# Weight-sum tables built in half-size pieces, one transfer at a time, in a two-layer decoder trunk on one core

## The chip, the core and the metric

The kernel runs on one core of a Trainium2 chip. The core has a matrix engine (TensorE, PE in the profile, with its weight loads listed as PEld), a vector engine (VectorE, DVE), a scalar engine (ScalarE, ACT), a general engine (GpSimd, POOL) and an engine that only issues transfers (SyncE, SP). Each runs its own list of instructions in order, and they meet through semaphores. Data comes from the chip's memory (DRAM) through 16 DMA engines, which all queues share: SP's transfers go through the queue that the profile calls q1, POOL's through q0.

The metric is the device time of one execution in microseconds, the median of several runs. Before the change it is 1178.66 us (three runs, 1177.95 to 1180.91).

## What is computed

The reference is a decoder trunk of two layers on 512 tokens of 1024 features, all in 32-bit floats. Layer 0 mixes with attention (8 forgetting-attention heads and 8 stick-breaking heads), layer 1 with a gated short convolution; each is followed by a gated MLP. Cut to its core:

```python
def conv_ffn(h, norm_g, w_up, conv_w, w_down):
    xn = rms_norm(h, norm_g)
    u = causal_dwconv(xn @ w_up, conv_w)
    g, val = u[..., :D_FF], u[..., D_FF:]
    return (jax.nn.silu(g) * val) @ w_down

def reference(x, ...):
    h = x
    for layer in range(DEPTH):              # DEPTH = 2
        i = layer // 2
        if layer % 2 == 0:
            h = h + attention_mixer(h, ...)
        else:
            h = h + short_conv_mixer(h, ...)
        h = h + conv_ffn(h, ffn_norm[layer], ffn_w_up[layer], ffn_conv[layer], ffn_w_down[layer])
    return h
```

`attention_mixer` is an input projection (`attn_w_in`, 1024 by 3080), normed queries and keys, two kinds of attention and an output projection (`attn_w_out`). D_FF is 2816, so `ffn_w_up` is 1024 by 5632.

## The kernel before

The program is one long stretch for each stage: attention (to about 300 us), the first MLP, the convolution mixer, the second MLP. Activations stay in SBUF; weights stream in from DRAM.

**Weights in attention.** `weights()` hands out the next weight tile (512 KB: 1024 rows by 128 columns, or 512 by 256). `load` has three buffers for the raw tile (`raw`) and three for its two halves `whi` and `wlo`, into which ACT (line 290) and DVE (line 291) split it, since each product is made of three passes of rounded halves (lines 311 to 313 for queries, keys and output). SP issues the load (line 284) as soon as a raw buffer is free, two tiles ahead of use. Heads and projections are woven together: a unit of a head (`logits`, `turn`, `weigh`, lines 605 to 830) alternates with pieces of the projections for later heads (`fillers`).

**Weights in the MLP.** The up projection multiplies 2 by 2 blocks of the matrix with seven products in place of eight (`Sevens`, line 1042 and around it). Some of these products need sums of weight blocks, named by the products p7, p6 and q4: the sum for p7 is the lower right block plus the upper right one, p6's is that plus the upper left, q4's that plus the lower left. For the second MLP these are added up on chip. For the first, columns 2 to 10 (groups of 256) have their sums ready in DRAM tables: nine tables, three sums (`"7"`, `"6"`, `"4"`) by three chunks of three groups, each 512 rows by 768 columns, 1.5 MB.

**How the tables are made.** `table_steps` is a generator that POOL's transfers come from. A step is one transfer from DRAM to DRAM: a plain copy (line 101), from the weights or from the table before, or a copy that adds onto what is there (line 99, `accum_op`). Six steps make the three tables of a chunk: copy and add for 7, copy and add for 6, copy and add for 4. The generator is called once ahead of attention's loop and then once a unit, and `pin` keeps its transfers in the order of the program among POOL's instructions. The scheduler puts the semaphores: a step waits until the step whose rows it reads or adds to has landed, and each eighth POOL transfer shares a counter.

**Who reads them.** In the first MLP, SP loads the 7 sum of a group into `Y` (line 1058), and the 6 and 4 sums into raw buffers (line 1066). POOL's next work behind the tables is a transfer that adds a block onto the tile `X` (line 1069), one for each group.

The loop that calls the generator, in the program of before:

```python
    sums_far = table_steps()
    next(sums_far)
    fill(PRE)
    for g in range(len(units) + 2):
        next(sums_far, None)
        if g < len(units):
            waiting[g] = logits(*units[g])
            fill(FILL1)
```

Of the kernel before, what the change touches and what calls it, by code (L numbers as in the profile page):

```python
# [22 lines left out]
ALU = mybir.AluOpType  # L23
# [26 lines left out]
CHUNKS = (2, 3), (5, 3), (8, 3)  # L50
# [4 lines left out]
def trunk(  # L55
# [6 lines left out]
    nc = tc.nc  # L62
# [20 lines left out]
    tables = {}  # L83

    def table_steps():

        w = ffn_w_up[0]
        for n in "764":
            for g, m in CHUNKS:
                tables[n, g] = far.tile([512, m * 256 + 16], F32, tag=f"t{n}{g}", name=f"t{n}{g}")  # L90
        def block(kh, half, g, m):
            return w[kh * 512:(kh + 1) * 512, half * DFF + g * 256:half * DFF + (g + m) * 256]
        for step in range(6):
            n = "764"[step // 2]
            for g, m in CHUNKS:
                to = tables[n, g][:, 0:m * 256]
                if step % 2:
                    src = block(*((0, 1), (0, 0), (1, 0))[step // 2], g, m)
                    pin(nc.gpsimd.dma_start(to, src, accum_op=ALU.add))
                else:  # L100
                    pin(nc.gpsimd.dma_start(to, block(1, 1, g, m) if step == 0 else tables["76"[step // 2 - 1], g][:, 0:m * 256]))
                yield

    def table_of(n, group):
        g, m = next(c for c in CHUNKS if c[0] <= group < c[0] + c[1])
# [120 lines left out]
    def fill(us):  # L226
        quota[0] += us
        while quota[0] > 0 and fillers:
            before = clock[0]
            if next(fillers[0], None) is None:  # L230
                fillers.pop(0)
            quota[0] -= clock[0] - before
# [15 lines left out]
    brought, pin = {}, tc.keep_in_program_order  # L248
# [486 lines left out]
    def turn(p, b, w):  # L735


        n = (b + 1) * P
        if b == 0:
            pts[p] = [aw.tile([P, 20, P], F32R, tag=f"pt{i}", name=f"pt{p}{i}", bufs=1) for i in range(2)]  # L740
        if b < 2:
            t = bank("c")
            for e in range(2):
                for k in range(b + 1):
                    c = (e * (b + 1) + k) * P
                    pe.transpose(t[:, c:c + P], w[:, e, k * P:(k + 1) * P], ident)
            src = t[:, 0:2 * n].rearrange("p (e n) -> p e n", e=2)
            if b:
                hi, lo = (t_[:, 4:20, :].rearrange("p (e k) q -> p e (k q)", e=2)[:, :, P:3 * P] for t_ in pts[p])
            else:  # L750
                hi, lo = (t_[:, 0:20:19, :] for t_ in pts[p])
            act.activation(hi, src, AF.Copy)
            dve.tensor_tensor(lo, src, f32(hi), op=ALU.subtract)
        else:
            for e in range(2):
                t = bank("c")
                for k in range(b + 1):
                    pe.transpose(t[:, k * P:(k + 1) * P], w[:, e, k * P:(k + 1) * P], ident)
                to = (5 * b, 19 - 6 * b)[e]
                hi, lo = (t_[:, to:to + b + 1, :].rearrange("p k q -> p (k q)") for t_ in pts[p])  # L760
                act.activation(hi, t[:, 0:n], AF.Copy)
                dve.tensor_tensor(lo, t[:, 0:n], f32(hi), op=ALU.subtract)
        spend(0.22 * (b + 1))

    def weigh(p):

        need(("v", p // 2))
        v = v_tiles[p // 2]  # L770
        if p == 4:
            o_tiles[1] = mixed(1)
        o_hi, o_lo = o_tiles[p // 4]
        total = work.tile([P, S], F32, tag="y", name=f"o{p}")
        for e in range(2):
            acc = bank("a")
            for k in range(NB):
                w = v[:, k, 2 * (p % 2) + e].rearrange("p i d -> p (i d)")
                first, step = ((6 * k, 5), (1 + k, 6))[e]
                out_ = acc[:, k * P:] if e == 0 else acc[:, 0:(NB - k) * P]  # L780
                for i, t in enumerate(pts[p]):
                    pe.matmul(out_, w, t[:, first:first + step * (NB - k - 1) + 1:step, :], start=k == 0 and i == 0, stop=k == NB - 1 and i == 1)  # L782
            src = acc.rearrange("p (b q) -> p b q", q=P)
            if e:
                src = src[:, ::-1, :]
            own, other = (slice(i * HD, (i + 1) * HD) for i in (e, 1 - e))
            to = total[own, :].rearrange("p (b q) -> p b q", q=P)
            act.activation(to, src[other], AF.Copy)
            dve.tensor_tensor(to, src[own], to, op=ALU.add)
            spend(1.2)  # L790
        split(o_hi[:, p % 4, :], o_lo[:, p % 4, :], total)

    def output(g, done):
        o_hi, o_lo = o_tiles[g]
        for o in range(ND):
            if o % 2 == 0:
                w = weights()
            acc = bank("a")
            c = slice((o % 2) * P, (o % 2 + 1) * P)
            for k in range(4):  # L800
                mm3(acc, (w[0][:, k, c], w[1][:, k, c]), (o_hi[:, k, :], o_lo[:, k, :]), k == 0, k == 3)
                yield 1
            done(o, acc)
# [15 lines left out]
    def output_begin():  # L819
        last_w.append([weights(), weights(AHEAD - 1)])  # L820
        yield from output_part(range(4), range(2), "b")
        last_w.append([weights(AHEAD - 1), weights(0)])
        yield from output_part(range(4), (2,), "b")
# [19 lines left out]
    rows = {}  # L843
# [95 lines left out]
    units = [(p, u) for p in range(8) for u in range(len(UNITS))]  # L939
    waiting = {}  # L940
    sums_far = table_steps()
    next(sums_far)
    fill(PRE)
    for g in range(len(units) + 2):
        next(sums_far, None)
        if g < len(units):
            waiting[g] = logits(*units[g])
            fill(FILL1)
        if g == len(units):
            fillers.append(output_begin())  # L950
            fill(BEFORE)
        if g >= 2 and units[g - 2][1] == len(UNITS) - 1:
            p = units[g - 2][0]
            weigh(p)
            if p == 3:
                fillers.append(output(0, residual))
        if 1 <= g <= len(units):
            for b, w in waiting.pop(g - 1):
                turn(units[g - 1][0], b, w)
                fill(FILL2 / len(UNITS[units[g - 1][1]]))  # L960
# [42 lines left out]
    class Blocks:  # L1003
# [15 lines left out]
        def block(self, name, k0, nk):  # L1019
            return self.at(k0 + (HF if name in "cd" else 0), nk)[:, :, LEFT if name in "ad" else RIGHT]  # L1020
# [662 lines left out]
```

## Time and profile before

| | |
|---|---|
| median of three runs | 1178.66 us (1177.95 to 1180.91) |
| the profiled execution | 1180.35 us, its span 1177.6 us |
| PE busy | 1132.7 us, 96% of the span |
| DVE, ACT, POOL busy | 949.4, 676.1, 138.8 us |
| mean granted clock of PE | 0.98 of full speed |
| moved by POOL's queue | 71.74 MB of 189.40 MB |
| chain that ended last | PE 82%, DMA 8%, DVE 4%, issue 2%, ACT 2% |

The profile comes from one execution. Its page cuts the span into 40 slices of 29.4 us and shows the busy share of each engine in tenths, the clock that PE was granted, and how full the DMA engines were. An answer by windows gives the same for chosen stretches in microseconds. An answer on waits says which engine stood still for whom. In an answer in order of time each row has its start and length, and in brackets the idle time before it with what ended it. "To landing" is the time from a transfer's issue to its last semaphore.

### The profile page before, as it was taken

Reading aid. Unit: us, or ns where it says so; the run is one execution under the profiler, and the core shown is the slowest. Engines: PE = TensorE matmul, PEld = TensorE weight load, DVE = VectorE, ACT = ScalarE, POOL = GpSimd, SP = SyncE. Lnnn points to the kernel's source line nnn. Section 1 sums busy time; section 2 is a strip of 40 time slices with the busy share of each in tenths; the row PEclk is TensorE's granted clock in tenths of the full one; section 3 lists DMA queues with packets and bytes.
Section 4 is the critical chain, followed back from the end, with each engine's and each line's share of the span. In section 5 each row is a group of like instructions: output and inputs, shape, how many; then the busy total and the mean of one; then the engine's idle time right before and its main releaser. Section 6 shows DMA issues by size and latency. Waiting matters only on the chain.

```text
span 1177.6 us, 19211 instructions
## 1 busy us (share of the span) xinstructions
PE 1132.7 (96%) x7619; PEld 1018.4 (86%) x7619; DVE 949.4 (81%) x1447; ACT 676.1 (57%) x1006; POOL 138.8 (12%) x156
## 2 busy tenths in 40 slices
PE   8987479999999999999999999999999999999998
PEld 7875358877888999999999889998888999998886
DVE  5764258988689978788998897885699899898886
ACT  7542246766456676667655644544354676766654
POOL 4101100000000111001420001000001111113300
PEclk9988689999999999999999999999999999999999
DMA  6799981212235787769994327543356786779961
GB/s 190 236 235 252 278 194 53 72 37 72 72 90 156 205 212 188 195 188 306 194 229 148 88 92 167 138 123 93 90 152 123 173 180 157 161 226 225 221 170 54
DMA packets 171401, 189.40 MB, mean 161 GB/s; under 512 B 6860, under 2 KB 140540, under 8 KB 171312
## 3 DMA queue, kind: packets, MB, share of 16 engines
q1 hardware_dynamic: 131712, 116.37, 32.1%
q0 software_dynamic: 39440, 71.74, 31.7%
q8 instruction: 59, 0.97, 0.3%
q14 instruction: 30, 0.25, 0.1%
q10 hardware_dynamic: 160, 0.07, 0.0%
HBM read 183.18 MB, written 30.41 MB: 181 GB/s over the span
## 4 chain that ended last, share of the span: by engine, by line
PE 82%; DMA 8%; DVE 4%; issue 2%; ACT 2%; another core or an unknown queue 1%; SPq 0%; DVEq 0%; ACTq 0%; POOLq 0%
PE psb L1042 23%; PE psb L1595 10%; PE psa L1042 9%; PE psa L1595 8%; DMA raw<-in_attn_w_in 7%; PE psb L311 5%; PE psb L313 4%; PE psb L312 4%; PE psa L311 3%; PE psa L313 3%; PE psa L312 3%; PE psa L782 2%; DMA Xc<-in_conv_w_in 1%; PE psb L686 1%; DVE wlo L291 1%
## 5 line engine op out<-in xcount | busy, mean ns | idle before, releaser
L290 ACT ACTIVATE whi<-raw 128x1024 fp32r<-128x1024 f32 (+2 forms) x93 | 95.9, 1033 | 140.4 <-DMA raw<-in_attn_w_in 51.0
L291 DVE TENSOR_TENSOR wlo<-raw,whi 128x1024 fp32r<-128x1024 f32 (+2 forms) x93 | 110.5, 1189 | 70.1 <-ACT whi L290 69.3
L1042 PE MATMUL psb<-p_lo,whi_p 128*128 128x256 f32 x408 | 115.0, 282 | 0.0
L1042 PE MATMUL psb<-p_hi,wlo_p 128*128 128x256 f32 x408 | 114.9, 282 | 0.0
L1042 PE MATMUL psb<-p_hi,whi_p 128*128 128x256 f32 x408 | 114.8, 281 | 0.0
L311 PE MATMUL psb<-hs_a,whi 128*128 128x512 f32 x240 | 101.1, 421 | 6.0 <-ACT qk L656 6.0
L313 PE MATMUL psb<-hs_a,wlo 128*128 128x512 f32 x240 | 97.0, 405 | 0.0
L1042 PEld LDWEIGHTS psb<-p_hi,whi_p 128*128 128x128 f32 x408 | 77.3, 190 | 0.0
L1042 PEld LDWEIGHTS psb<-p_lo,whi_p 128*128 128x128 f32 x408 | 76.9, 189 | 0.0
L1042 PE MATMUL psa<-p_hi,wlo_p 128*128 128x256 f32 x272 | 76.8, 282 | 0.0
L1042 PE MATMUL psa<-p_lo,whi_p 128*128 128x256 f32 x272 | 76.7, 282 | 0.0
L1042 PE MATMUL psb<-q_lo,whi_q 128*128 128x256 f32 x272 | 76.6, 282 | 0.0
L1042 PEld LDWEIGHTS psb<-p_hi,wlo_p 128*128 128x128 f32 x408 | 76.6, 188 | 0.0
L1042 PE MATMUL psb<-q_hi,wlo_q 128*128 128x256 f32 x272 | 76.6, 281 | 0.0
L1042 PE MATMUL psb<-q_hi,whi_q 128*128 128x256 f32 x272 | 76.5, 281 | 0.0
L1042 PE MATMUL psa<-p_hi,whi_p 128*128 128x256 f32 x272 | 76.5, 281 | 0.0
L1069 POOL DMA_DIRECT2D X<-in_ffn_w_up x17 | 22.3, 1313 | 375.3 <-DVE wlo_p L992 274.2
L1595 PE MATMUL psb<-act,whi 128*128 128x256 f32 x352 | 63.3, 282 | 0.0
L311 PEld LDWEIGHTS psb<-hs_a,whi 128*128 128x128 f32 x240 | 46.8, 195 | 16.3 <-ACT qk L656 6.4
L421 DVE SCALAR_TENSOR_TENSOR uv<-yv,taps,uv 128x511 f32<-128x511 f32 (+1 forms) x84 | 59.8, 746 | 0.2
L421 DVE SCALAR_TENSOR_TENSOR ug<-yg,taps,ug 128x511 f32<-128x511 f32 (+1 forms) x84 | 58.9, 747 | 0.3 <-ACT ug L418 0.3
L1595 PE MATMUL psb<-whi,act 128*128 128x512 f32 x176 | 56.6, 398 | 0.0
(480 smaller groups left out, 3678.3 us busy)
## 6 DMA issues: line engine op xcount, KB each, us to landing
t<-in_ffn_w_up POOLq DMA_DIRECT2D x12, 1536.0 KB, 20.4
raw<-in_attn_w_in SPq DMA_DIRECT2D x24, 512.0 KB, 5.8
raw<-in_ffn_w_up SPq DMA_DIRECT2D x20, 512.0 KB, 3.9
t<-t POOLq DMA_DIRECT2D x6, 1536.0 KB, 19.1
X<-in_ffn_w_up SPq DMA_DIRECT2D x17, 512.0 KB, 5.0
W<-in_ffn_w_up SPq DMA_DIRECT2D x17, 512.0 KB, 4.7
X<-in_ffn_w_up POOLq DMA_DIRECT2D x17, 512.0 KB, 7.5
Z<-in_ffn_w_up SPq DMA_DIRECT2D x17, 512.0 KB, 4.4
```

The lines of the kernel that those rows point to most:

```text
L290: return (act.activation(hi[:, at_], raw[:, at_], AF.Copy), dve.tensor_tensor(lo[:, at_], raw[:, at_], f32(hi[:, at_]), op=ALU.subtract))
L291: dve.tensor_tensor(lo[:, at_], raw[:, at_], f32(hi[:, at_]), op=ALU.subtract))
L311: made = [pe.matmul(acc, w[0], rhs[0], start=first, stop=False), pe.matmul(acc, w[0], rhs[1], start=False, stop=False), pe.matmul(acc, w[1 ...
L312: pe.matmul(acc, w[0], rhs[1], start=False, stop=False),
L313: pe.matmul(acc, w[1], rhs[0], start=False, stop=last)]
L421: dve.scalar_tensor_tensor(dst[:, d:], src[:, 0:S - d], tap(j), dst[:, d:], op0=ALU.mult, op1=ALU.add)
L686: pe.matmul(ss[e][:, c:c + wide], ql[rows, b * P:n], kl[rows, 0:wide], start=first and b == bs[0], stop=last and b == bs[-1])
L782: pe.matmul(out_, w, t[:, first:first + step * (NB - k - 1) + 1:step, :], start=k == 0 and i == 0, stop=k == NB - 1 and i == 1)
L1042: pe.matmul(to, w[a][:, k, c], x[b][:, k, :], start=fresh and i + k + t == 0, stop=i == 1 and k == 3 and t == 2, skip_group_check=not fresh)
L1069: tc.keep_in_program_order(nc.gpsimd.dma_start(self.st[g][n], self.block_of(g, kh, half), accum_op=ALU.add))
L1595: pe.matmul(to, l, r, start=begin and o + t == 0, stop=end and t == 2 and o == (0 if layer else 1), skip_group_check=not fresh)
```

## The change

The same nine tables are made with the same sums. Each transfer now covers 256 of a table's 512 rows (0.75 MB), so there are 36 in place of 18. The loops change places: before, a step was made for all three chunks before the next step; now all six steps are made for the upper rows of a chunk, then for its lower rows, then the next chunk follows. In this order each transfer but the first of six reads or adds to what the one in front of it wrote. The loop over attention's units asks for two steps a turn.

```diff
-        for step in range(6):
-            n = "764"[step // 2]
-            for g, m in CHUNKS:
-                to = tables[n, g][:, 0:m * 256]
-                if step % 2:
-                    src = block(*((0, 1), (0, 0), (1, 0))[step // 2], g, m)
-                    pin(nc.gpsimd.dma_start(to, src, accum_op=ALU.add))
-                else:
-                    pin(nc.gpsimd.dma_start(to, block(1, 1, g, m) if step == 0 else tables["76"[step // 2 - 1], g][:, 0:m * 256]))
-                yield
+        for g, m in CHUNKS:
+            for rows in (slice(0, 256), slice(256, 512)):
+                for step in range(6):
+                    n = "764"[step // 2]
+                    to = tables[n, g][rows, 0:m * 256]
+                    if step % 2:
+                        src = block(*((0, 1), (0, 0), (1, 0))[step // 2], g, m)
+                        pin(nc.gpsimd.dma_start(to, src[rows, :], accum_op=ALU.add))
+                    else:
+                        src = block(1, 1, g, m) if step == 0 else tables["76"[step // 2 - 1], g][:, 0:m * 256]
+                        pin(nc.gpsimd.dma_start(to, src[rows, :]))
+                    yield
...
     for g in range(len(units) + 2):
-        next(sums_far, None)
+        for _ in range(2):
+            next(sums_far, None)
         if g < len(units):
```

## The prediction, made before the result was known

> **What bounds the kernel now.** I read the slices of the page first, then the waits of the worst stretch, the chain, the DMA queues, and last GpSimd's (POOL's) own order of time. The slices, each 29.4 us wide:
>
> ```profile
> span 1177.6 us, 19211 instructions
> ...
> PE   8987479999999999999999999999999999999998
> ...
> PEclk9988689999999999999999999999999999999999
> DMA  6799981212235787769994327543356786779961
> ```
>
> The kernel is bound by TensorE (PE) almost everywhere; the one hole is in slices 2 to 5, about 60 to 177 us. There the DMA engines are full and, with PE's busy share, its granted clock falls. Three stretches, before, in and after the hole (columns: length, busy time of PE, PEld, DVE, ACT and POOL with the number of instructions, granted clock, DMA share, GB/s):
>
> ```profile
> 40.00:68.00 28.00, 28.00 (x174) 22.10 (x173) 22.88 (x61) 15.12 (x33) 5.54 (x7) 1.00 1.04 281
> 68.00:180.00 112.00, 77.41 (x463) 61.98 (x463) 51.30 (x126) 40.17 (x92) 10.30 (x12) 0.79 1.00 239
> 180.00:306.00 126.00, 123.37 (x806) 101.87 (x803) 109.15 (x224) 81.80 (x160) 0.00 (x0) 1.00 0.19 58
> ```
>
> All three are the same attention code (heads, value projections, fillers). In the second PE is idle 112.00 - 77.41 = 34.6 us, in the third 126.00 - 123.37 = 2.6 us, or 2.1%. DVE and ACT are busy less than half of the second stretch, so neither is its limit. The waits of 68 to 180 us (who waited for whom, us in total, times, longest):
>
> ```profile
> ACT whi L290 <- DMA raw<-in_attn_w_in: 51.0, 5, 12.9
> PE psc L605 <- ACT sq L648: 9.1, 1, 9.1
> PE psb L686 <- ACT w L704: 8.0, 2, 7.7
> PE psc L638 <- DVE pt L762: 7.0, 1, 7.0
> PE psb L311 <- ACT qk L656: 6.0, 1, 6.0
> ```
>
> ACT splits every weight tile (line 290), works in order, and stands 51 us in front of tiles that have not landed; PE's waits name what is queued on ACT and DVE behind that split. The chain of work that ended last says it more plainly (start, us, what):
>
> ```profile
> 46.05 25.32 DMA raw<-in_attn_w_in
> ...
> 95.93 46.89 DMA raw<-in_attn_w_in
> ```
>
> A weight tile of 0.5 MB is on the chain for 47 us. The DMA queues of 46 to 172 us, when the tables are made, and then the loads of 180 to 306 us, when none are:
>
> ```profile
> q0 software_dynamic: 7013, 27.16, 89.0%
> q1 hardware_dynamic: 8291, 4.70, 15.7%
> ...
> t<-in_ffn_w_up POOLq DMA_DIRECT2D x9, 1536.0 KB, 22.3
> t<-t POOLq DMA_DIRECT2D x6, 1536.0 KB, 19.1
> raw<-in_attn_w_in SPq DMA_DIRECT2D x9, 512.0 KB, 44.5
> ```
> ```profile
> raw<-in_attn_w_in SPq DMA_DIRECT2D x4, 512.0 KB, 3.8
> ```
>
> The table transfers (queue q0) and the weight tiles (q1) move nearly the same number of packets, 7013 against 8291, but 27.16 MB against 4.70. The engines take turns packet by packet, and q0's packets are large (27.16 MB / 7013 = 3.9 KB, against 0.6 KB). With q0 never empty, a tile lands after 44.5 us (median) instead of 3.8, and nine tiles in 126 us is one in 14. So the hole is the weight tiles' queue behind tables that nobody needs before 355 us.
>
> **The change, part by part.** POOL's order before, from the first table on (DMASWn is a counter that every eighth POOL transfer raises; a transfer waits for its own counter's last use and for its data):
>
> ```order
> L101 DMA t_599<-in_ffn_w_up 512x768 [waits DMASW4_49]
> L101 DMA t_600<-in_ffn_w_up 512x768 [waits DMASW5_49]
> L101 DMA t_601<-in_ffn_w_up 512x768 [waits DMASW6_49]
> L99 DMA t_599<-in_ffn_w_up 512x768 [waits DMASW7_49,DMASW4_49]
> L99 DMA t_600<-in_ffn_w_up 512x768 [waits DMASW5_49,DMASW0_49]
> ```
>
> and after:
>
> ```order
> L103 DMA t_599<-in_ffn_w_up 256x768 [waits DMASW4_49]
> L100 DMA t_599<-in_ffn_w_up 256x768 [waits DMASW5_49,DMASW4_49]
> L103 DMA t_602<-t_599 256x768 [waits DMASW6_49,DMASW5_49]
> L100 DMA t_602<-in_ffn_w_up 256x768 [waits DMASW7_49,DMASW6_49]
> L103 DMA t_605<-t_602 256x768 [waits DMASW7_49,DMASW0_49]
> L100 DMA t_605<-in_ffn_w_up 256x768 [waits DMASW1_49,DMASW0_49]
> L103 DMA t_599<-in_ffn_w_up 256x768 [waits DMASW2_49]
> ```
>
> Three chunks were interleaved, so two transfers always stood behind the one under way. Now six steps on the same rows follow each other, and each waits for its predecessor's counter. Only the first of each later six (five places) has nothing to wait for but a counter long raised, and goes out with the one before. On PE, DVE, ACT and SP the rows stay the same, in the same order; on POOL 18 rows become 36. POOL in order of time before (start, us, what, idle before it and its releaser):
>
> ```profile
> 40.51 1.92 POOL L101 DMA_DIRECT2D t<-in_ffn_w_up  x3
> 49.87 1.11 POOL L99 DMA_DIRECT2D t<-in_ffn_w_up  x1 [7.44 <-DMA t<-in_ffn_w_up]
> 55.15 1.03 POOL L99 DMA_DIRECT2D t<-in_ffn_w_up  x1 [4.18 <-DMA t<-in_ffn_w_up]
> 60.56 1.01 POOL L99 DMA_DIRECT2D t<-in_ffn_w_up  x1 [4.38 <-DMA t<-in_ffn_w_up]
> 69.44 0.66 POOL L101 DMA_DIRECT2D t<-t  x1 [7.86 <-DMA t<-in_ffn_w_up]
> 77.83 0.64 POOL L101 DMA_DIRECT2D t<-t  x1 [7.74 <-DMA t<-in_ffn_w_up]
> 86.98 0.63 POOL L101 DMA_DIRECT2D t<-t  x1 [8.50 <-DMA t<-in_ffn_w_up]
> ...
> 142.87 1.00 POOL L99 DMA_DIRECT2D t<-in_ffn_w_up  x1 [3.14 <-DMA t<-t]
> 371.70 1.35 POOL L1069 DMA_DIRECT2D X<-in_ffn_w_up  x1 [227.82 <-DVE wlo_p L992]
> ```
>
> *How long the new chain takes.* With the queue full, copies land 5.3 us apart (49.87, 55.15, 60.56) and adds about 8.9 (60.56, 69.44, 77.83, 86.98). Halves then stream 2.65 and 4.45 us. The first copy was alone at its start: 49.87 - 40.51 = 9.4 us from issue to the next issue, less 5.3 of streaming: 4.1 us of fixed cost that the full queue hid and each wait now shows. So a pair is 2.65 + 4.45 + 2 x 4.1 = 15.3 us, eighteen pairs 275 us, less 5 x 4.1 where two go together: 255 us, from 40.5 to about 295 us instead of 170. No row shows the fixed cost of a lone half, so its bounds:
>
> ```profile
> spare<-in_ffn_conv POOLq DMA_DIRECT2D x4, 33.0 KB, 2.0
> ```
> ```profile
> p_lo_chain<-in_ffn_w_down POOLq DMA_DIRECT2D x6, 512.0 KB, 10.0
> ```
>
> Below, 2.0 us, a transfer of next to nothing: the chain ends at 40.5 + 128 + 31 x 2.0 = 230 us. Above, an add of 0.5 MB in the crowded down projection, 10.0 less a third of 8.9: 7.0 us, end at 385. I take 4.1, since it is the same transfer at the same place.
>
> *Who waits for POOL.* Until 371.70 nothing else of POOL is due. The last table is issued at 164 + 30F for a fixed cost F, 287 us with 4.1. The order shows the X transfer right behind it:
>
> ```order
> L103 DMA t_607<-t_604 256x768 [waits DMASW5_49]
> L100 DMA t_607<-in_ffn_w_up 256x768 [waits DMASW6_49]
> L1072 DMA X_3694<-in_ffn_w_up 128x4x256 [waits DMAHW7_49,DVE_49]
> ```
>
> It comes due about 45 us earlier than before, at 326, so POOL is free 39 us ahead. The tables' readers (first and last start):
>
> ```profile
> L1058 SPq DMA_DIRECT2D Y<-t x9: 367/499/508, 355.7 to 504.7; - x9
> ```
>
> Nine groups 18.6 us apart; the three chunks, first read at 356, 411 and 467, would be read at 311, 366 and 422 and be whole at about 128, 212 and 295. The halved transfers' own issues are free beside POOL's 227.82 us of idleness; only if the chain ran past 326 would that cover be gone.
>
> *What PE gets back.* First its idleness, 34.6 us. Then the clock: the five pieces of the hole at half clock are
>
> ```profile
> 72.73:79.55 6.82, 5.43 (x43) 4.20 (x44) 4.11 (x9) 3.94 (x12) 0.64 (x1) 0.52 1.09 214
> 106.90:117.10 10.20, 5.76 (x28) 4.63 (x29) 4.47 (x9) 3.26 (x7) 0.92 (x1) 0.51 1.09 213
> 123.90:134.20 10.30, 7.20 (x22) 5.09 (x23) 4.78 (x12) 4.93 (x13) 0.95 (x2) 0.51 1.05 348
> 137.60:151.20 13.60, 6.68 (x27) 5.33 (x28) 6.30 (x16) 5.94 (x12) 2.03 (x2) 0.51 1.05 236
> 164.90:171.70 6.80, 4.75 (x17) 3.99 (x17) 4.88 (x10) 2.96 (x9) 0.00 (x0) 0.52 0.98 258
> ```
>
> PE is busy 29.8 of these 47.7 us, and half of that, 14.9, is the clock's. Together 49.5; the work left, 112 - 49.5 = 62.5 us, keeps the 2.1% of the calm stretch: -1.3. The Trainium skill, TensorE: Matmul & The Clock Gate, Terms, sets the penalty at the throttled time times one half, which would put 23.9 us in place of 14.9 and end at 1125 us. The rows differ, because the remaining 17.9 us of those pieces are idle and counted already; I keep 14.9.
>
> *What the tiles still lose.* In each gap of 4.1 us q0 is empty, and a tile alone lands in 3.8; in a pair's 15.3 us that is two tiles, and the 7.1 us of streaming carry another half at one in 14. So a tile each 6 us at the least, where PE at full pace wants nine in 62.5 us, one in 7. A tile issued just as an add starts lands after about 4.45 + 3.8 = 8.3 us. Three buffers run ahead, but tiles come in bursts. Between nothing, as at 40 to 68 us, where PE never stood under a full queue, and 1 us for each of some 22 tiles up to 295 us, I take 3 us: nearer the lower end, since even 25.32 us of lateness cost little before 73 us.
>
> The saving is 34.6 + 14.9 - 1.3 - 3 = 45 us. The rest of the program only moves ahead. The profiled execution took 1180.35 us, 2.75 around its span; it becomes 1135. It lay 1.7 above the median shown, 1178.66; against that the forecast is 1134.
>
> **The rivals.** (a) *Half of it stays:* the tables crowd the tiles for 255 us rather than 130, and each of the 22 tiles costs its 1 us or more: 22 us in place of 3, about 1153. For it, the calm stretch now gets a rival queue; against it, the gaps. (b) *POOL comes late:* the chain's last issue at 164 + 30F reaches 326 at F = 5.4 us, after which X, and with it the weights of every group, are late by 30 us for each us of F. At 6.9 nothing is left of the saving, at 8 the kernel takes 1212. For it speaks the 10.0 us row; against it 9.4 us for twice the copy. The Trainium skill, SBUF — State Buffer, SBUF: two separate sides, says that certain VectorE operations lock GpSimd out while it writes descriptors, 620 ns becoming 3100; by that F would be 6.6 and the time about 1170. The issues at 40.51 took 1.92 for three beside a DVE busy 22.88 of 28 us, so the trace does not show it. (c) *The tables were not the cause:* ACT's and DVE's own chain binds 68 to 180 us, and the time stays near 1175; against it, the third stretch, 98% busy with the same code. (d) *The change doesn't do what it says:* the five pairs in flight make a full queue of 7.1 us at most, too little to matter.
>
> **How the numbers follow.** Forecast (1129 to 1142): 0.77. (a), 1142 to 1165: 0.13. (c): 0.03, of which 0.01 unmoved. (b): 0.07, of which 0.05 slower, 0.01 unmoved and 0.01 faster. (d): none. The range 1127 to 1156 takes the forecast and most of (a), since its loss is the term with no row. A change of 0.3%, 3.5 us, is about what can be told from none. Faster 0.93, same 0.02, slower 0.05.
>
> **What would show it.** Right: weight tiles landing in 4 to 9 us between 46 and 290 us, PE over 95% busy at full clock there, ACT's wait for raw under 8 us, tables issued until 280 to 300 us, and the first Y read from a table near 311 us. Wrong: POOL's last table after 326 us, or raw still over 15 us to landing.

## The result

The changed kernel takes 1131.07 us (median of four runs, 1129.42 to 1131.6) against 1178.31 us for the kernel before, measured beside it: a ratio of 0.9595 (95% interval 0.9574 to 0.9615), 47 us saved. The forecast was 1134 us, range 1127 to 1156. In the profiled execution the span went from 1177.6 to 1127.5 us.

The slices of the page after, each 28.2 us wide:

```profile
span 1127.5 us, 19238 instructions
...
PE   8999999999999999999999999999999999999998
...
PEclk9999999999999999999999999999999999999999
DMA  6678767674368777799953455543275876789961
```

The hole in slices 2 to 5 (counted from 0) is gone, the granted clock does not fall, and the DMA engines are busy six to eight tenths up to slice 8 instead of nearly full in slices 2 to 5. (Lines of the program after the edit stand two to three lower: the split of a weight tile, 290 and 291 before, is now 292 and 293, and the X transfer, 1069 before, is 1072.) The same stretches, with the columns of the prediction:

```profile
40.00:68.00 28.00, 28.00 (x173) 22.08 (x172) 23.03 (x62) 16.29 (x34) 4.14 (x6) 1.00 0.81 203
68.00:180.00 112.00, 111.42 (x794) 92.78 (x793) 93.21 (x225) 73.71 (x162) 13.35 (x18) 1.00 0.78 190
180.00:261.00 81.00, 78.37 (x487) 63.65 (x484) 68.31 (x127) 47.86 (x92) 9.68 (x13) 1.00 0.72 179
```

From 68 to 180 us PE runs 794 matmuls where it ran 463, and is idle 0.6 us where it was idle 34.6. The DMA queues of 46 to 172 us after:

```profile
q0 software_dynamic: 4346, 16.30, 57.7%
q1 hardware_dynamic: 11984, 6.82, 19.5%
...
raw<-in_attn_w_in SPq DMA_DIRECT2D x14, 512.0 KB, 5.0
```

In the same 126 us the tables move 16.30 MB instead of 27.16, and the weight tiles' queue 11984 packets instead of 8291. A tile lands after 5.0 us (median) instead of 44.5, and fourteen are fetched instead of nine. POOL in order of time, at the chain's start and end:

```profile
40.30 0.58 POOL L103 DMA_DIRECT2D t<-in_ffn_w_up  x1
46.94 0.99 POOL L100 DMA_DIRECT2D t<-in_ffn_w_up  x1 [6.05 <-DMA t<-in_ffn_w_up]
54.81 0.58 POOL L103 DMA_DIRECT2D t<-t  x1 [6.88 <-DMA t<-in_ffn_w_up]
59.50 0.99 POOL L100 DMA_DIRECT2D t<-in_ffn_w_up  x1 [4.11 <-DMA t<-t]
...
257.60 0.89 POOL L100 DMA_DIRECT2D t<-in_ffn_w_up  x1 [6.24 <-DMA t<-t]
323.37 1.35 POOL L1072 DMA_DIRECT2D X<-in_ffn_w_up  x1 [64.88 <-DVE wlo_p L995]
```

The last table is issued 66 us ahead of POOL's next work.

### The profile page after: what moved, and what is told of

Read it like the earlier page. It is cut to its first block, busy times and chain, and to the rows that moved or that the text cites. A ratio compares the mean times of both kernels' runs of the same rounds, so it can differ in the third digit from the quotient of the medians.

```text
span 1127.5 us, 19238 instructions
## 1 busy us (share of the span) xinstructions
PE 1116.9 (99%) x7619; PEld 1007.1 (89%) x7619; DVE 948.9 (84%) x1447; ACT 674.8 (60%) x1006; POOL 150.3 (13%) x174
## 4 chain that ended last, share of the span: by engine, by line
PE 90%; DVE 5%; ACT 2%; DMA 2%; issue 1%; DVEq 0%; ACTq 0%; POOLq 0%
PE psb L1045 23%; PE psb L1598 11%; PE psa L1045 9%; PE psa L1598 8%; PE psb L313 6%; PE psb L314 6%; PE psb L315 6%; PE psa L315 3%; PE psa L313 3%; PE psa L314 3%; DMA Xc<-in_conv_w_in 2%; PE psa L784 2%; PE psb L688 2%; PE psb L570 1%; PE psb L571 1%
## 5 line engine op out<-in xcount | busy, mean ns | idle before, releaser
L313 PE MATMUL psb<-hs_a,whi 128*128 128x512 f32 x240 | 98.5, 410 | 0.0
L1598 PEld LDWEIGHTS psb<-act,whi 128*128 128x128 f32 x352 | 54.2, 189 | 0.5 <-DVE act L995 0.3
L315 PEld LDWEIGHTS psb<-hs_a,wlo 128*128 128x128 f32 x240 | 45.1, 188 | 10.5 <-DVE wlo L293 0.2
```

The costliest lines, as they stand in the source:

```text
L313: made = [pe.matmul(acc, w[0], rhs[0], start=first, stop=False), pe.matmul(acc, w[0], rhs[1], start=False, stop=False), pe.matmul(acc, w[1 ...
L315: pe.matmul(acc, w[1], rhs[0], start=False, stop=last)]
L1598: pe.matmul(to, l, r, start=begin and o + t == 0, stop=end and t == 2 and o == (0 if layer else 1), skip_group_check=not fresh)
```

## The experiments

The change does three things at once: it halves the transfers, puts them chunk by chunk, and so leaves one in flight. The runs take these apart, and then ask what it is about the queue that delays a weight tile. All kernels keep the instructions of PE, ACT, DVE and SP in the same order; only POOL's table transfers differ. Each was timed beside the kernel before on the same chip.

**The changed kernel again.**

> The changed kernel once more, beside the variants on the same chip. Both theories: about 1131 us, ratio 0.96 to the kernel before; weight tiles land in about 5 us while the tables are made, and PE stays over 98% busy from 68 to 261 us.

Measured: 1130.62 us against 1177.74, ratio 0.9602 (0.9584 to 0.9619). It is the yardstick of the three that follow.

**The order alone, whole tables.** Against the changed kernel:

```diff
-            for rows in (slice(0, 256), slice(256, 512)):
+            for rows in (slice(0, 512),):
...
-        for _ in range(2):
-            next(sums_far, None)
+        next(sums_far, None)
```

> The new order alone: six steps on a chunk, each waiting for the one in front of it, but with whole tables of 1.5 MB, 18 transfers. Theory A (what counts is that POOL's queue runs empty between two transfers, and a weight tile gets through in that gap): the gap is there, only half as often; a copy and an add stream 13 us and leave two gaps of about 3 us, room for four tiles in 19 us. 1131 to 1138 us, tiles landing in 5 to 12 us, tables done near 210 us. Theory B (what counts is the size of a transfer, since a tile has to stand behind a whole one): a tile waits up to 9 us more behind an add, and a good part of the loss comes back: 1145 to 1165 us.

Measured: 1130.75 us, ratio 0.9606 (0.9589 to 0.9624): the whole saving, with transfers as large as before. Its DMA queues of 46 to 172 us and the stretch of 68 to 180 us:

```profile
q0 software_dynamic: 5100, 19.98, 64.8%
q1 hardware_dynamic: 11956, 6.80, 20.7%
...
raw<-in_attn_w_in SPq DMA_DIRECT2D x14, 512.0 KB, 7.9
```
```profile
68.00:180.00 112.00, 111.46 (x794) 92.81 (x792) 93.31 (x225) 73.67 (x162) 10.29 (x12) 1.00 0.88 218
```

Tiles land later, after 7.9 us, and it costs PE nothing. Theory B, that size decides, falls here.

**The halves alone, in the old order.** Against the changed kernel:

```diff
-        for g, m in CHUNKS:
-            for rows in (slice(0, 256), slice(256, 512)):
-                for step in range(6):
+        for step in range(6):
+            for g, m in CHUNKS:
+                for rows in (slice(0, 256), slice(256, 512)):
```

> The halves alone: 36 transfers of 0.75 MB in the old order, step by step over all three chunks, so that five more stand behind the one under way. Theory A: the queue never runs empty, tiles land after 40 us or more, the time is that of before, 1175 to 1182 us. Theory B: with half the size a tile waits half as long, and half of the saving is there, about 1155 us.

Measured: 1174.47 us, ratio 0.9971 (0.9960 to 0.9982), a saving of 3 us, half a microsecond beyond theory A's 1175 to 1182 and far from theory B's 1155.

```profile
q0 software_dynamic: 7301, 27.25, 87.4%
q1 hardware_dynamic: 9053, 5.09, 16.9%
...
raw<-in_attn_w_in SPq DMA_DIRECT2D x10, 512.0 KB, 40.7
```
```profile
68.00:180.00 112.00, 82.98 (x499) 66.84 (x497) 56.65 (x150) 43.68 (x100) 16.78 (x23) 0.82 0.98 238
```

The hole is back, with tiles at 40.7 us. So the halving by itself is worth 3 us, and the order by itself all of the saving.

**Two halves in flight.** Against the changed kernel:

```diff
-            for rows in (slice(0, 256), slice(256, 512)):
-                for step in range(6):
+            for step in range(6):
+                for rows in (slice(0, 256), slice(256, 512)):
```

> The halves of a chunk made side by side: upper rows and lower rows of each step, then the next step, so two transfers of 0.75 MB are in flight. Theory A: while one half's wait runs (about 3 us), the other streams (2.1 us a copy, 4.5 us an add), so the queue is empty only for a moment around the copies; tiles land in 12 to 30 us, tables done near 185 us, and 1145 to 1175 us. Theory B: transfers as small as in the changed kernel, so the time of the changed kernel, 1131 to 1136 us.

Measured: 1132.16 us, ratio 0.9616 (0.9601 to 0.9630). Theory A's number was wrong here: tiles landed after 9.1 us, not 12 to 30, and PE lost nothing. The number of theory B, 1131 to 1136 us, came out, although the two runs before had already refuted that size alone decides.

```profile
q0 software_dynamic: 6602, 24.87, 82.5%
q1 hardware_dynamic: 12018, 6.85, 19.0%
...
raw<-in_attn_w_in SPq DMA_DIRECT2D x14, 512.0 KB, 9.1
```

The tables are done at 189 us, not much later than the 170 of before. Either short empty moments are enough, or it is the amount in front of a tile that counts. The next two runs were meant to part these.

**Four quarters in flight**, as many bytes as two halves. Against the changed kernel:

```diff
-            for rows in (slice(0, 256), slice(256, 512)):
-                for step in range(6):
+            for step in range(6):
+                for rows in (slice(r, r + 128) for r in range(0, 512, 128)):
...
-        for _ in range(2):
+        for _ in range(4):
```

> Chunk by chunk, each step cut into four quarters of 0.375 MB that are issued together, then the next step: as many bytes in flight (1.5 MB) as with two halves, but while one quarter waits out its fixed cost of about 3 us, three others stream (6.6 us of adds, 3.2 us of copies), so that the queue hardly ever runs empty. Theory A (the empty moments let the tiles through): tiles land after 25 to 45 us again, PE stands idle 20 to 35 us between 68 and 180 us, and the time is 1160 to 1178 us. Theory C (the bytes or the transfers that stand in front of a tile count, and 1.5 MB is little enough): tiles land in about 9 us as with two halves, and the time is 1131 to 1136 us.

Measured: 1132.36 us, ratio 0.9618 (0.9601 to 0.9635). Theory A's number missed again, and that of theory C, 1131 to 1136 us, came out.

```profile
q0 software_dynamic: 7451, 26.14, 83.3%
q1 hardware_dynamic: 11972, 6.81, 19.6%
...
raw<-in_attn_w_in SPq DMA_DIRECT2D x14, 512.0 KB, 11.5
```

What I had taken for a queue that hardly ever runs empty was low often enough. Its tile queue moved 4521 packets more than the table queue; in the kernel before, whose table queue is full until its last table lands at 170 us, the surplus was 1278. A tile of queries or keys is 1024 rows of 512 bytes, so these are about three tiles more that got through beside the turns that the two queues take, and PE, which wants fourteen in this stage and got nine in the kernel before and ten with the halves alone, is no longer starved. The packets of the trace show when: in the kernel before, with both queues full, each begins some 50 to 60 packets a microsecond; here the table queue falls at times to half of that or less, and the tile queue then begins up to 470. The queue need not be empty on all engines at once for this: no table packet at all was under way for only 1.4 of the 126 us, against 44.6 in the changed kernel.

**Narrow rows, with the old order and the full queue.** Against the kernel before:

```diff
-                to = tables[n, g][:, 0:m * 256]
-                if step % 2:
-                    src = block(*((0, 1), (0, 0), (1, 0))[step // 2], g, m)
-                    pin(nc.gpsimd.dma_start(to, src, accum_op=ALU.add))
-                else:
-                    pin(nc.gpsimd.dma_start(to, block(1, 1, g, m) if step == 0 else tables["76"[step // 2 - 1], g][:, 0:m * 256]))
+                for j in range(m):
+                    c = slice(j * 256, (j + 1) * 256)
+                    to = tables[n, g][:, c]
+                    if step % 2:
+                        src = block(*((0, 1), (0, 0), (1, 0))[step // 2], g, m)
+                        pin(nc.gpsimd.dma_start(to, src[:, c], accum_op=ALU.add))
+                    else:
+                        src = block(1, 1, g, m) if step == 0 else tables["76"[step // 2 - 1], g][:, 0:m * 256]
+                        pin(nc.gpsimd.dma_start(to, src[:, c]))
```

> The kernel before with its order, its three chunks in turn and its full queue, but each transfer cut by columns into three of 256 columns, so that a row is 1 KB instead of 3 KB; the same bytes in 54 transfers. Theory A', that the engines take turns packet by packet: a tile's 64 packets per engine now stand behind 64 packets of a third of the length, it is served in 8 to 9 us instead of 14 to 18, close to the 7 us that PE wants; tiles land in 15 to 30 us, most of the idle time goes, 1135 to 1155 us, with a queue that is never empty. Rival, that a full queue delays tiles by its bytes, whatever their packets: tiles after 40 us and more, 1172 to 1180 us.

Measured: 1131.98 us, ratio 0.9614 (0.9594 to 0.9634), better than the 1135 to 1155 of theory A'.

```profile
q0 software_dynamic: 16299, 25.80, 91.2%
q1 hardware_dynamic: 11619, 6.46, 23.0%
...
t<-in_ffn_w_up POOLq DMA_DIRECT2D x28, 512.0 KB, 23.0
t<-t POOLq DMA_DIRECT2D x18, 512.0 KB, 17.5
raw<-in_attn_w_in SPq DMA_DIRECT2D x14, 512.0 KB, 15.4
```

The table queue is as full as before (91.2%, and its own transfers land after 17 to 23 us), it moved nearly the same bytes, and about as much stands in front of a tile; but its packets average 1.6 KB instead of 3.9 (12281 of 1 KB and 3229 of 4 KB, where the kernel before had 4608 of 3 KB and 2117 of 6 KB). The turns can be counted where both queues have work all the time. The queues from 60 to 80 us, first in the kernel before, then here:

```profile
q0 software_dynamic: 1212, 3.63, 93.2%
q1 hardware_dynamic: 1213, 0.61, 15.4%
```
```profile
q0 software_dynamic: 2755, 2.74, 84.7%
q1 hardware_dynamic: 2754, 1.39, 34.7%
```

In both, the two queues begin the same number of packets, to within one, whatever the bytes. With the smaller table packets the turns come more than twice as fast, and the tiles get 1.39 MB instead of 0.61. So turns by packets are shown; theory C, that the bytes or transfers in front count, does not fit this run.

**Whole tables, two in flight, then one.** Against the order alone:

```diff
-        for g, m in CHUNKS:
-            for rows in (slice(0, 512),):
-                for step in range(6):
+        for chunks in (CHUNKS[:2], CHUNKS[2:]):
+            for step in range(6):
+                for g, m in chunks:
```

> Whole tables of 1.5 MB, those of the first two chunks side by side (two in flight), then those of the third chunk alone (one in flight). While one table's fixed cost of 3 to 4 us runs, the other streams 4.2 us (copy) or 8.9 us (add), so that the queue is never empty until the third chunk begins near 125 us. Theory A'' (turns by packets: with 6912 table packets in all, the fourteen tiles that PE wants in this stage, 14336 packets, get through only where the queue is empty for about 12 us in total): up to 125 us tiles land after 20 to 40 us, PE stands idle 10 to 20 us, afterwards they land in 4 to 16 us; 1142 to 1158 us. Rival D (two in flight is few enough, whatever their size): as with two halves, tiles after about 9 us, 1130 to 1135 us.

Measured: 1141.20 us, with more spread than the others (1137.33 to 1145.86), ratio 0.9693 (0.9659 to 0.9728). That is 10 us above the order alone, just under the range of theory A'' and above that of rival D. The loads of 46 to 125 us, then of 125 to 190 us, and PE's stretch from 68 to 128 us:

```profile
raw<-in_attn_w_in SPq DMA_DIRECT2D x8, 512.0 KB, 23.0
```
```profile
raw<-in_attn_w_in SPq DMA_DIRECT2D x6, 512.0 KB, 9.0
```
```profile
68.00:128.00 60.00, 53.72 (x383) 43.94 (x381) 41.81 (x107) 32.35 (x76) 6.91 (x8) 1.00 1.07 271
```

With two in flight the size does count. The working had it that a whole table streams longer than the other's fixed cost, so that the queue never empties. That was too strong: from 46 to 113 us the tile queue got ahead of the table queue in 14 of 67 us, fewer than the 22 with two halves, but not none (the table under "The cause"). Why two whole tables leave fewer such moments than two halves is argued, not shown. Idleness came to 6.3 us here instead of the 10 to 20 expected.

**Quarters, one in flight.** Against the changed kernel:

```diff
-            for rows in (slice(0, 256), slice(256, 512)):
+            for rows in (slice(r, r + 128) for r in range(0, 512, 128)):
...
-        for _ in range(2):
+        for _ in range(4):
```

> The changed kernel with quarters (0.375 MB, 72 transfers), still one in flight: the fixed cost is paid 61 times. With 128 us of streaming and 3.1 us each, as the changed kernel's chain of 225 us gives, the last table is issued near 353 us, 30 us after the point (323 us) at which POOL's first X transfer is due behind it. If X and what it feeds stand on the path, as the prediction's case of a late POOL has it: PE idle some 25 to 30 us near 330 us, 1155 to 1162 us. If there is room behind X: under 10 us lost, 1131 to 1141 us. Tiles land in 4 to 6 us in both.

Measured: 1167.91 us, ratio 0.9928 (0.9905 to 0.9951): 37 us slower than the changed kernel, though its tiles land soonest (after 4.3 us, median of the fourteen from 46 to 172 us). POOL in order of time, the waits of ACT and PE from 290 to 420 us, and the stretch itself:

```profile
359.21 0.82 POOL L100 DMA_DIRECT2D t<-in_ffn_w_up  x1 [3.40 <-DMA t<-t]
360.71 1.36 POOL L1072 DMA_DIRECT2D X<-in_ffn_w_up  x1 [0.68 <-issue]
```
```profile
ACT whi_q L993 <- DMA X<-in_ffn_w_up: 35.7, 1, 35.7
PE psb L1045 <- ACT Xs L1097: 33.7, 1, 33.7
```
```profile
300.00:420.00 120.00, 86.28 (x609) 81.41 (x608) 78.47 (x108) 55.05 (x73) 20.33 (x23) 0.86 0.70 173
```

X goes out at 360.71 where it was due at 323.37, 37 us late; ACT waits for it, PE for what ACT makes next, and the kernel loses 37 us. There is no room behind X. The expected 1155 to 1162 was short because the last table was issued at 359.21, 6 us later than worked out, and because the lateness cost its full length.

## Why the prediction was right

**The cause.** That the tiles' queue behind the tables makes the hole, and not ACT's or DVE's own chain (rival c), is shown: with the tables out of the way PE is 99.5% busy from 68 to 180 us, and every kernel whose tiles land after a median of 16 us or less reaches 1130.6 to 1132.4 us, but for the quarters, whose POOL came late. With the two whole tables, where the median of the first eight was 23 us, part of the loss stays. How the tiles get through can be counted from the packets of each trace, microsecond by microsecond from 46 to 113 us, when all these kernels make tables:

| kernel | us of 67 in which the tile queue began over 1.5 times the table queue's packets | tile packets | loss against the changed kernel, us |
|---|---|---|---|
| before | 0 | 3479 | 47 |
| halves alone | 0 | 3703 | 43 |
| whole tables, two in flight | 14 | 6163 | 10 |
| two halves in flight | 22 | 7168 | 1 |
| four quarters in flight | 25 | 6935 | 1 |
| whole tables, one in flight | 23 | 7168 | 0 |
| changed kernel | 23 | 7168 | 0 |
| narrow rows, full queue | 0 | 6171 | 1 |

The last row has no such moments at all, and gets its tiles by shorter turns. It moved no more tile packets in this time than the two whole tables, but more evenly: its eight tiles issued in these 67 us landed after 14.8 to 21.5 us, those of the two whole tables after 10.4 to 33.0, and ACT stood 4.5 us in front of tiles up to 180 us where it stood 14.2 up to 128.

**What PE got back.** The two terms, idleness of 34.6 and 14.9 for the clock, make 49.5; the spans differ by 50.1, the medians by 47.2. The clock's term can be set against three more runs by the same working, idle time plus half of the busy time at half clock, summed over 40 to 420 us from the instructions and clock records of each trace, and taken relative to the changed kernel's 3.2 us:

| kernel | idle | at half clock | of it busy | idle + half busy - 3.2 | its span - 1127.5 |
|---|---|---|---|---|---|
| before | 37.2 | 47.8 | 28.6 | 48.3 | 50.1 |
| halves alone | 31.7 | 41.0 | 27.5 | 42.2 | 44.5 |
| quarters, one in flight | 36.9 | 34.1 | 4.9 | 36.2 | 39.3 |
| whole tables, two in flight | 9.7 | 6.8 | 5.9 | 9.4 | 10.3 |

With half of all the time at half clock, as the Trainium skill has it (TensorE: Matmul & The Clock Gate, Terms), these would be, by an estimate from its rule, 57.9, 49.0, 50.8 and 9.9. The first three traces go against adding that to the idle time, the quarters most of all: there nearly all the time at half clock was one wait. In the fourth PE was busy in nearly all of it, and the two workings hardly differ. What the first working leaves over, 1 to 3 us, is no more than the spans of kernels with the same 3.2 us differ by (1127.5 to 1130.6).

**The mis-sized terms.** Two deductions of the sum, 1.3 us for the calm stretch's idleness and 3 for late tiles, came out at almost nothing: 0.6 us of idleness in 112. Without them the forecast would have been 1130.

The chain of tables was put at 255 us and took 225, its last landing at 265 us instead of 295. The first copy fitted (6.6 us from issue to issue, 6.75 forecast), the first add took 7.9 for 8.55, the copy from table to table 4.7 for 6.75. The step that failed is the fixed cost of 4.1 us. The three chains with one transfer in flight show it: from the first issue to the last landing they took 177 us with whole tables (16 waits), 225 with halves (31) and 324 with quarters (61), so that each further wait cost 3.2 to 3.3 us and about 125 us are left for the streams, which were put at 128. The 4.1 came from one copy that was taken to be alone, but from 38 to 48 us the weight tiles' queue moved 1.55 MB beside it. The chain was hidden work, so its 30 us of error cost the forecast nothing here; with quarters the same sum decided.

**The rivals.** A late POOL (b) was named with its place and its price, and the quarters show both: 37 us late, 37 us lost. The changed kernel stays 66 us clear of it, where I had worked out 39. The longer issues that (b) also weighed did not come: the 36 took 0.58 to 0.99 us each, beside a DVE busy 93.21 of 112 us. That half of the loss might stay (a) did not happen, since even tiles at 15 us cost PE less than 1 us (idleness of 1.3 us from 68 to 180 us with narrow rows, 0.6 in the changed kernel). The prediction gave the emptiness between transfers as the reason that tiles get through; it is one of two sufficient ones, the other being smaller packets.

Of the signs named beforehand, tiles at 4 to 9 us (median 5.0), PE at full clock and over 95% busy, and ACT without a wait for raw from 68 to 180 us came true, and the first Y was read from a table at 307.4 us, near the 311 forecast. The last table issue, 257.6 us, missed its 280 to 300.

## What to carry to other kernels

Transfers that nobody needs soon should not keep a queue full beside loads that are needed now: chain them so that the queue empties now and then, or give them shorter rows (here 1 KB was enough beside loads with rows of 512 bytes, and 3 KB was not), and count the turns (packets) that both sides want in the stage. Before going smaller, add up the fixed costs of the chain and look at what is queued behind it on the issuing engine; here halving on top of the new order cost nothing and gained nothing, quartering lost most of the gain.

## What was not expected

How little emptiness is enough: two halves or four quarters in flight leave the tables' queue 82 to 83% busy instead of 89%, and the median tile goes from 44.5 us to 9.1 or 11.5. And the full queue with rows of 1 KB, the same work in the old order, does as well as the change itself (ratio 0.9614 against 0.9595, with intervals that overlap).
